# Second attention layer: the two parts of the output joined by VectorE out of PSUM

## The chip, the cores and the metric

The kernel runs on one core of one Trainium2 chip. The metric is the device time of one execution in microseconds. Three runs of the kernel before took 2756.7, 2753.62 and 2752.54 us; the median is 2753.62 us. One more execution was recorded by the hardware profiler: it took 2757.76 us, and the span from its first to its last instruction is 2756.0 us.

## The reference

All data are float32, the sequence has 1024 rows of 1024 channels. The reference computes a two-layer transformer block and then a state-space and convolution block. Each transformer layer is `x = x + g1 * attention(h)` and `x = x + g2 * swiglu(h)`, where `h` is an RMS norm of `x`, scaled and shifted by values that come from a conditioning vector.

The first layer has windowed attention (16 query heads, 4 key heads). The second, which the change touches, has dilated attention: three groups of 8 query heads and 2 key heads of 64 channels, with windows of 128, 512 and 2048 rows and dilations of 1, 4 and 16:

```python
for gi, (window, dil) in enumerate(B_GROUPS):
    half = window // (2 * dil)
    o, lse = banded_attention(to_strided(q[:, :, gi], dil), ...)
    outs.append(from_strided(o, b, dil)); lses.append(from_strided(lse, b, dil))
alpha = jax.nn.softmax(jnp.stack(lses), axis=0)
o = jnp.einsum('nbshg,nbshgd->bshgd', alpha, jnp.stack(outs))
```

Within a group each query attends to the keys at most `half` steps away in the strided sequence, with a bias that falls with the distance. The three groups' outputs are then weighed by the softmax of their log denominators, and a matrix multiplication follows.

## The kernel before

The program is one instruction stream per engine. The parts run one after the other: attention layer A, feed-forward 0, attention layer B (`layer_b`), feed-forward 1, the last block. Float32 products are made from operands split into a high part in the rounded format fp32r and the rest (`hi`, `lo`), so a projection is three matrix multiplications per tile (L590 to L592, into PSUM tiles `psg`), and a cast by ScalarE and a subtraction by VectorE make each split.

Layer B works through six units in the order of group 2, 1, 0 (dilations 16, 4, 1), two halves of the heads each. A unit has eight blocks of 128 queries for four heads, 48 blocks in all. A block goes through these steps (class `Block`, function `attend`):

- `score`: per head two matrix multiplications (L113, L114) into a PSUM bank of the two called `pssc`; VectorE adds the bias and takes the row maximum (L117), which frees the bank. After the fourth head VectorE scales the maxima (L122, 128x4).
- `soft`: ScalarE takes the exponential (L126) of each head, which needs L122.
- `turn`, one block later: TensorE transposes the four heads' weights P (L756) into a bank `pstp`; ScalarE casts the high part (L759), VectorE subtracts for the low part (L760).
- `apply`, also one block later (function `pv`): TensorE multiplies with the values (L770) into the only bank `pso`. The values stand there as high part and low part side by side, so the result has two parts: partitions 0 to 63 and 64 to 127 have to be added. ScalarE copies partitions 64 to 127 to an SBUF tile `ob` (L773) and partitions 0 to 63 to the output tile `o` (L779); GpSimd adds `ob` to `o` in place (L780).

The output tile holds a head's rows in their own order. In group 0 a block's 128 queries are 128 neighbours there. In group 1 they lie 4 elements apart and in group 2 16 apart, so the output of L779 is strided in the first four units and contiguous in the last two.

Between the steps `attend` calls `fill`, which issues pieces of the next unit's projections: the matrix multiplications, ScalarE's casts of the queries (L682), keys and values (L644 to L646, L659), VectorE's subtractions (L686, L648, L649, L660), and the next weights: a load on SyncE's queue (L544), a cast by ScalarE (L536), a subtraction by GpSimd (L537). The casts and subtractions of the queries and keys write strided in groups 2 and 1.

The outputs of groups 2 and 1 go to DRAM by SyncE when a unit is done (`spill`, L1125). Near the end of the layer the function `combine` (L1018 to L1060) reads them back and weighs the groups for one half of the rows, in small steps between the last blocks (L1031 and L1034 among them); the steps for the other half follow during the output projection.

The order on each engine's queue is not the written one. The program is traced, and the framework's scheduler sets the order of every queue at build time by what its own model of the run finds ready, what is written first being preferred; the run then keeps that order. Semaphores make an instruction wait, and what is behind it on its engine's queue waits with it. The function `pin` and the context `in_order` hold single places to the written order; layer B's blocks use neither.

The change touches the class `Net`'s start, the end of `pv`, and one line in `build`.

Of the kernel before, what the change touches and what calls it, by code (L numbers as in the profile page):

```python
# [32 lines left out]
class Steps:  # L33


    def __init__(self, gen):
        self.gen, self.value, self.live = gen, None, True
# [111 lines left out]
class Net:  # L149
    def __init__(self, tc, I, out, dbg=None):  # L150
        self.tc, self.nc, self.I, self.out = tc, tc.nc, I, out
        self.dbg = dbg or {}
        self.n = 0
        self.ready = {}
        self.spread_tag, self.sum_tag, self.ada_tag = "o", "r", "g"

    def nm(self, s):
# [476 lines left out]
    def kv_proj(self, W, h, perm, res):  # L634

        nc = self.nc
        K1, K2 = self.slab(dt=F32R, name="K1"), self.slab(dt=F32R, name="K2")
        vt = self.slab("tmp", name="vt")
        res.update(K1=K1, K2=K2, vt=vt)
        for hf in range(2):  # L640
            ps = self.bank("g")
            yield from self.col_gemm_steps(ps, W(), h, hf)
            pk, pv = perm(ps[0:64], None), perm(ps[64:128], None)
            nc.scalar.copy(perm(K1[0:64], hf), pk)  # L644
            nc.scalar.copy(perm(K1[64:128], hf), pk)
            nc.scalar.copy(perm(vt[64:128], hf), pv)  # L646
            yield
            nc.vector.tensor_sub(perm(K2[0:64], hf), pk, perm(fl(K1[0:64]), hf))  # L648
            nc.vector.tensor_sub(perm(K2[64:128], hf), pk, perm(fl(K1[0:64]), hf))  # L649
# [113 lines left out]
    def pv(self, pairs, oap, r0):  # L763

        nc = self.nc
        po = self.bank("o")
        n = len(pairs)
        for a, (v, pt) in enumerate(pairs):
            for part in range(2):
                nc.tensor.matmul(po, v, pt[:, part, :], start=(a == 0 and part == 0),  # L770
                                 stop=(a == n - 1 and part == 1))
        ob = self.small([P, H2], "ob", 2)[r0:r0 + 64]
        nc.scalar.copy(ob, po[64:128, :])  # L773
        a = po[0:64].rearrange("p (i q) -> p i q", i=4)
        b = ob.rearrange("p (i q) -> p i q", i=4)
        if len(oap.shape) == 4:
            r = oap.shape[2]
            a, b = [t.rearrange("p i (r q) -> p i r q", r=r) for t in (a, b)]
        nc.scalar.copy(oap, a)  # L779
        nc.gpsimd.tensor_add(oap, oap, b)  # L780

    def layer_a(self, h, late, then):
        nc, I = self.nc, self.I
# [1177 lines left out]
def build(tc, I, out, dbg=None, stop=None):  # L1961
    with ExitStack() as ctx:
        net, nc = Net(tc, I, out, dbg), tc.nc
        net.open(ctx)
        net.consts()
        net.load_vectors()
        xd, xd1 = net.spill_tile(), net.spill_tile()
        x0 = net.load_x(0)
        w1 = [net.ada_load(0, 1, k, "slab") for k in range(KT)]
        x1 = net.load_x(1)  # L1970
        w0 = [net.ada_load(0, 0, k, "slab") for k in range(KT)]
        net.x = Act(net, "x")
        with net.in_order():
            h, half = net.norm(net.x, lambda v: net.mod[0, 0] if v else s, rows=(x0, x1))
            first, second = Steps(half(0)), Steps(half(1))
            first.run(4)
            net.turn_x(0, x0)
            first.run(12)
            acc = net.ada_acc(w1)
            net.ada_fin(0, 1, acc)  # L1980
            s = net.ada_scale(0, 1, net.nmix[:, 0:8])
            first.run(1)
            second.run(4)
            net.turn_x(1, x1)
            acc = None
            for k in range(KT):
                acc = net.ada_acc(w0[:k + 1], acc, k)
                if k < 6:
                    second.run(2)
            for n, parts in enumerate(([(1024, 64), (1280, 64)], [(0, P)])):  # L1990
                net.ready[n] = net.load_cols(I["a_w_in"][0], parts, eng=nc.gpsimd)
            net.ada_fin(0, 0, acc)
            first.run()
            second.run()
        net.pending = second
        for hf in range(2):
            net.spill_x(xd, hf)
        net.half = {}

        def ffn_norm(i):  # L2000
            s2 = net.ada_scale(i, 4, net.nffn[:, 8 * i:8 * i + 8])
            net.H, half = net.block_norm(net.x, lambda v: net.mod[i, 3] if v else s2, lambda hf: net.spill_x(xd, hf))
            return half

        def b_norm():
            s = net.ada_scale(1, 1, net.nmix[:, 8:16])
            net.h, half = net.norm(net.x, lambda v: net.mod[1, 0] if v else s, ("s", "slab"))

            def both(hf, order=range(KT)):
                for n, _ in enumerate(half(hf, order)):  # L2010
                    if n == KT - 1:
                        net.spill_x(xd1, hf)
                    yield
            return both

        net.layer_a(h, lambda: net.reload_x(xd, True), lambda: ffn_norm(0))
        if stop == "A":
            return net.dump_x()
        early, late = net.ssm_params()
        net.ada_tag = "o"  # L2020
        d = net.ffn_wide(0, net.H, Steps(net.adas([(1, 1), (1, 0), (1, 2), (1, 4), (1, 3)], "wl")))
        net.ffn_narrow(0, d, xd, b_norm, early)
        if stop == "F0":
            return net.dump_x()
        net.layer_b(net.h, lambda: net.reload_x(xd1), lambda: ffn_norm(1))
        if stop == "B":
            return net.dump_x()
        d = net.ffn_wide(1, net.H, Steps(net.adas([(1, 5)], "wl")))
        net.ffn_narrow(1, d, xd, net.mix_norm, late)
        if stop == "F1":  # L2030
            return net.dump_x()
        net.mixer2()
# [41 lines left out]
```

## Time and profile before

| | before |
|---|---|
| median of three runs | 2753.62 us |
| the profiled execution's own time | 2757.76 us |
| its span | 2756.0 us |
| TensorE busy (matrix multiplications) | 2593.1 us, 94% |
| VectorE busy | 1899.1 us, 69% |
| ScalarE busy | 1286.1 us, 47% |
| GpSimd busy | 376.4 us, 14% |
| DMA, mean over the span | 122 GB/s |

Busy time is the time in which an engine works on an instruction; time in which it waits for a semaphore is idle. The shares are averages over stages of different kinds. In the rows further down, PE is TensorE's matrix multiplication and PEld its weight load, DVE is VectorE, ACT ScalarE, POOL GpSimd and SP SyncE. `out<-in` names the tiles that an instruction writes and reads, L779 is line 779 of the kernel, and a bracket such as `[1.08 <-PE pssc L114]` says how long the engine was idle before the instruction and which instruction ended that time. In a list of waits, the instruction on the left waited for the one on the right.

### The profile page before, as it was taken

The page shows a single profiled execution, that of the slowest core. Times are in us where ns is not written, and L with a number is a line of the kernel's source. Part 1 is how long each engine was busy: PE and PEld are TensorE (multiplying, and loading weights), DVE is VectorE, ACT ScalarE, POOL GpSimd, SP SyncE. Part 2 cuts the span into 40 slices and gives each one's busy share as a digit, 9 for nine tenths or more (in the row PEclk, how much of TensorE's full clock was granted, in tenths as well). Part 3 has the DMA queues.
Part 4 walks back from the last instruction along what each step waited for, and adds up shares of the span by engine and source line. Part 5 has one row for each costly group of instructions (what it writes and reads, how often), then busy time and mean ns, then how long its engine had stood idle before and what let it go on. Part 6 is the DMA issues. An engine that isn't in the chain of part 4 may idle for free. (4 is left out here: it accounts for less than half of the span.)

```text
span 2756.0 us, 33954 instructions
## 1 busy us (share of the span) xinstructions
PE 2593.1 (94%) x11966; PEld 2115.1 (77%) x11966; DVE 1899.1 (69%) x3559; ACT 1286.1 (47%) x2416; POOL 376.4 (14%) x506
## 2 busy tenths in 40 slices
PE   4999998999999999988899889999999899999998
PEld 4777676888888788776787668888887777988877
DVE  7788777977775976755667798666656978165355
ACT  4577743433333345568888443333333445123131
POOL 2255521000000000023343200000000102020000
PEclk8999999999999999999999999999999999999999
DMA  7333341544444666311122414222274565161141
GB/s 276 99 93 96 119 123 69 156 142 146 138 138 139 232 200 194 107 39 40 39 55 78 145 59 146 82 86 83 85 244 150 176 199 175 54 180 52 46 144 63
DMA packets 283403, 336.74 MB, mean 122 GB/s; under 512 B 59384, under 2 KB 212704, under 8 KB 282592
## 3 DMA queue, kind: packets, MB, share of 16 engines
q1 hardware_dynamic: 277520, 315.59, 36.4%
q0 software_dynamic: 5312, 18.88, 2.1%
q8 instruction: 94, 1.54, 0.2%
q14 instruction: 77, 0.63, 0.1%
q10 hardware_dynamic: 400, 0.09, 0.0%
HBM read 265.14 MB, written 67.27 MB: 121 GB/s over the span
## 5 line engine op out<-in xcount | busy, mean ns | idle before, releaser
L1188 PE MATMUL psg<-H,wpart 128*128 128x512 f32 x2112 | 504.6, 393 | 14.3 <-ACT H L432 10.0
L1188 PEld LDWEIGHTS psg<-H,wpart 128*128 128x128 f32 x2112 | 397.8, 189 | 103.6 <-ACT H L432 12.8
L1175 ACT CAST wpart<-wraw 128x512 fp32r<-128x512 f32 x264 | 163.3, 622 | 248.3 <-PE pstp L1188 76.4
L1188 PE MATMUL pssc<-H,wpart 128*128 128x512 f32 x1056 | 255.0, 390 | 0.5 <-DVE ev L1208 0.5
L1188 PEld LDWEIGHTS pssc<-H,wpart 128*128 128x128 f32 x1056 | 198.1, 188 | 42.1 <-DVE ev L1208 0.9
L1176 DVE TENSOR_TENSOR wpart<-wraw,wpart 128x512 fp32r<-128x512 f32 x264 | 180.9, 686 | 68.5 <-ACT wpart L1175 66.7
L1325 PE MATMUL psg<-part,wpart 128*128 128x512 f32 x792 | 206.8, 394 | 8.0 <-DVE wpart L1291 3.1
L1325 PE MATMUL pssc<-part,wpart 128*128 128x512 f32 x792 | 207.4, 394 | 5.2 <-DVE ev L1212 3.6
L590 PE MATMUL psg<-hh,wh 128*128 128x512 f32 x480 | 198.5, 414 | 2.2 <-ACT hh L527 1.7
L1290 ACT CAST wpart<-wraw 128x640 fp32r<-128x640 f32 (+1 forms) x132 | 101.0, 765 | 210.7 <-PE psg L1325 101.8
L591 PE MATMUL psg<-hl,wh 128*128 128x512 f32 x480 | 192.6, 401 | 2.0 <-DVE hl L530 1.9
L592 PE MATMUL psg<-hh,wl 128*128 128x512 f32 x480 | 191.8, 400 | 0.0
L1325 PEld LDWEIGHTS psg<-part,wpart 128*128 128x128 f32 x792 | 148.4, 189 | 42.7 <-DVE part L1297 5.5
L126 ACT ACTIVATE s<-s,nm 128x256 f32<-128x256 f32 (+4 forms) x320 | 162.4, 511 | 39.6 <-DVE nm L122 33.1
L1325 PEld LDWEIGHTS pssc<-part,wpart 128*128 128x128 f32 x792 | 148.3, 189 | 39.4 <-DVE ev L1212 4.3
L1291 DVE TENSOR_TENSOR wpart<-wraw,wpart 128x640 fp32r<-128x640 f32 (+1 forms) x132 | 117.7, 892 | 83.4 <-ACT wpart L1290 75.8
L1203 ACT COPY ev<-psg 128x512 f32<-128x512 f32 x132 | 77.4, 588 | 205.1 <-PE psg L1188 141.0
L780 POOL TENSOR_TENSOR o<-o,ob 64x512 f32<-64x512 f32 x80 | 117.3, 1467 | 231.8 <-ACT o L779 221.6
L403 POOL TENSOR_TENSOR nacc<-nacc,nsq 128x512 f32<-128x512 f32 x30 | 40.5, 1350 | 761.8 <-ACT nsq L401 761.5
L1325 PE MATMUL pstp<-part,wpart 128*128 128x512 f32 x528 | 137.9, 393 | 0.0
L1296 ACT CAST part<-a 128x512 fp32r<-128x512 f32 x176 | 108.5, 618 | 58.0 <-PE pssc L1325 17.7
L1297 DVE TENSOR_TENSOR part<-a,part 128x512 fp32r<-128x512 f32 x176 | 119.6, 691 | 19.0 <-ACT part L1296 17.8
(454 smaller groups left out, 5488.8 us busy)
## 6 DMA issues: line engine op xcount, KB each, us to landing
adaw<-in_ada_w_dram SPq DMA_DIRECT2D x96, 512.0 KB, 4.2
wraw<-in_ffn_w_in_dram SPq DMA_DIRECT2D x88, 512.0 KB, 3.9
a<-acts SPq DMA_DIRECT2D x132, 256.0 KB, 4.0
acts<-ev SPq DMA_DIRECT2D x44, 512.0 KB, 2.7
wraw<-in_ffn_w_out_dram SPq DMA_DIRECT2D x44, 384.0 KB, 3.5
xs<-x SPq DMA_DIRECT2D x32, 512.0 KB, 3.5
x<-xs SPq DMA_DIRECT2D x32, 512.0 KB, 5.1
wraw<-in_ffn_w_out_dram SPq DMA_DIRECT2D x44, 320.0 KB, 3.3
```

Source lines behind the costliest of these rows:

```text
L126: self.net.nc.scalar.activation(s[:, 0:w], s[:, 0:w], AF.Exp, bias=self.nm[:, i:i + 1], scale=0.125, accum_out=self.l[:, i:i + 1])
L590: nc.tensor.matmul(ps, hi[:, k, :], xhi, start=(k == 0), stop=False)
L591: nc.tensor.matmul(ps, hi[:, k, :], xlo, start=False, stop=False)
L592: nc.tensor.matmul(ps, lo[:, k, :], xhi, start=False, stop=(k == KT - 1))
L780: nc.gpsimd.tensor_add(oap, oap, b)
L1175: nc.scalar.copy(t[:, lo_half], src)
L1176: nc.vector.tensor_sub(t[:, hi_half], src, fl(t[:, lo_half]))
L1188: nc.tensor.matmul(bank[q, key], a[:, ks], b, start=first and k == m == 0, stop=k == 3 and m == 2, skip_group_check=not first)
L1291: nc.vector.tensor_sub(lo, t[:, 0:n], fl(hi))
L1296: nc.scalar.copy(o[:, lo_half], a)
L1297: nc.vector.tensor_sub(o[:, hi_half], a, fl(o[:, lo_half]))
L1325: nc.tensor.matmul(banks[m], a[:, ms], b, start=k == n == 0, stop=k == NK - 1 and n == 2)
```

## The change

A switch `sum_here` is added. `build` sets it before layer B, and from then on `pv` issues one VectorE addition of the two parts, the first read from PSUM and the second from `ob`, written to the output tile, in place of ScalarE's copy and GpSimd's addition. ScalarE's copy to `ob` stays. Layer A keeps the old form.

```diff
--- before.py
+++ after.py
@@ -152,6 +152,7 @@
         self.dbg = dbg or {}
         self.n = 0
         self.ready = {}
+        self.sum_here = False
         self.spread_tag, self.sum_tag, self.ada_tag = "o", "r", "g"
 
     def nm(self, s):
@@ -776,8 +777,11 @@
         if len(oap.shape) == 4:
             r = oap.shape[2]
             a, b = [t.rearrange("p i (r q) -> p i r q", r=r) for t in (a, b)]
-        nc.scalar.copy(oap, a)
-        nc.gpsimd.tensor_add(oap, oap, b)
+        if self.sum_here:
+            nc.vector.tensor_add(oap, a, b)
+        else:
+            nc.scalar.copy(oap, a)
+            nc.gpsimd.tensor_add(oap, oap, b)
 
     def layer_a(self, h, late, then):
         nc, I = self.nc, self.I
@@ -2022,6 +2026,7 @@
         net.ffn_narrow(0, d, xd, b_norm, early)
         if stop == "F0":
             return net.dump_x()
+        net.sum_here = True
         net.layer_b(net.h, lambda: net.reload_x(xd1), lambda: ffn_norm(1))
         if stop == "B":
             return net.dump_x()
```

## Rows read from the trace of the kernel before

**Rows 1.** Busy time of each engine in two stretches: the blocks of layer B, and the end of the layer. Columns: stretch, its length, busy us (and instructions) of PE, PEld, DVE, ACT and POOL, granted clock of TensorE, DMA share, GB/s.

```profile
1193.00:1545.00 352.00, 319.07 (x1649) 254.63 (x1648) 226.67 (x609) 284.19 (x661) 116.36 (x87) 0.98 0.22 54
...
1528.00:1545.00 17.00, 14.66 (x56) 8.72 (x56) 14.86 (x25) 9.08 (x22) 4.35 (x3) 1.00 0.50 169
```

**Rows 2.** The three longest waits of TensorE's matrix multiplications, 1193 to 1545 us. Columns: who waited for whom, us in total, times, longest us.

```profile
PE pso L770 <- DVE pt L760: 9.1, 12, 1.7
PE pssc L113 <- DVE st L117: 9.1, 10, 2.2
PE pso L770 <- ACT pt L759: 5.2, 9, 1.5
```

**Rows 3.** Instructions of one line: count, shortest, median and longest duration in ns, first and last start in us. L779 in groups 2 and 1 and then in group 0 (the first of its 17 is still of group 1), L686 in the first units and in the last, and L122 in layer B.

```profile
L779 ACT COPY o<-pso x31: 1012/1050/1092, 1204.8 to 1436.1; 64x512 f32<-64x512 f32 x31
...
L779 ACT COPY o<-pso x17: 577/581/1072, 1441.5 to 1539.7; 64x512 f32<-64x512 f32 x17
...
L686 DVE TENSOR_TENSOR Q<-psg,Q x16: 1007/1073/1106, 1169.1 to 1253.2; 64x512 fp32r<-64x512 f32 x16
...
L686 DVE TENSOR_TENSOR Q<-psg,Q x8: 683/689/694, 1472.0 to 1512.8; 64x512 fp32r<-64x512 f32 x8
...
L122 DVE TENSOR_SCALAR nm<-st x48: 150/484/3579, 1194.3 to 1527.1; 128x4 f32<-128x4 f32 x48
```

**Rows 4.** The group of GpSimd's additions, 1193 to 1545 us. Columns: count, busy us, mean ns of one, idle us before them and what ended it.

```profile
L780 POOL TENSOR_TENSOR o<-o,ob 64x512 f32<-64x512 f32 x48 | 71.1, 1481 | 209.0 <-ACT o L779 199.6 <-PE pstp L756 5.8 <-PE pssc L114 3.5
```

**Rows 5.** Timeline of VectorE, ScalarE and GpSimd in the block at 1390 us. Columns, here and below: start us, us, engine, line and operation, idle time before it.

```profile
1391.11 0.42 DVE L117 CUSTOM_DVE_ANT_0 s<-pssc,bias 128x256 f32<-128x256 f32 x1
...
1392.62 0.42 DVE L117 CUSTOM_DVE_ANT_0 s<-pssc,bias 128x256 f32<-128x256 f32 x1 [1.08 <-PE pssc L114]
...
1390.58 0.58 ACT L773 COPY ob<-pso 64x512 f32<-64x512 f32 x1 [0.21 <-PE pso L770]
...
1393.29 1.08 ACT L759 CAST pt<-pstp 128x512 fp32r<-128x512 f32 x2 [1.06 <-PE pstp L756]
...
1392.37 1.57 POOL L780 TENSOR_TENSOR o<-o,ob 64x512 f32<-64x512 f32 x1 [5.06 <-ACT o L779]
```

**Rows 6.** Timeline of the four engines in the block at 1226 us.

```profile
1228.71 3.58 DVE L122 TENSOR_SCALAR nm<-st 128x4 f32<-128x4 f32 x1
...
1233.36 0.69 DVE L760 TENSOR_TENSOR pt<-pstp,pt 128x512 fp32r<-128x512 f32 x1
...
1227.23 1.03 ACT L779 COPY o<-pso 64x512 f32<-64x512 f32 x1
1228.06 1.06 ACT L536 CAST wh<-wr 128x1024 fp32r<-128x1024 f32 x1
1229.03 2.21 ACT L682 CAST Q<-psg 64x512 fp32r<-64x512 f32 x2
1231.26 0.59 ACT L759 CAST pt<-pstp 128x512 fp32r<-128x512 f32 x1
...
1228.34 1.58 POOL L780 TENSOR_TENSOR o<-o,ob 64x512 f32<-64x512 f32 x1 [3.50 <-PE pssc L114]
1229.88 2.38 POOL L537 TENSOR_TENSOR wl<-wr,wh 128x1024 fp32r<-128x1024 f32 x1
...
1231.90 0.51 PE L770 MATMUL pso<-pt,V 128*128 128x512 f32 x1 [0.37 <-ACT pt L759]
...
1234.11 0.50 PE L770 MATMUL pso<-pt,V 128*128 128x512 f32 x1 [1.71 <-DVE pt L760]
```

**Rows 7.** Timeline of TensorE in five more blocks: matrix multiplications of L770 that waited for a half of the split.

```profile
1264.60 0.50 PE L770 MATMUL pso<-pt,V 128*128 128x512 f32 x1 [0.57 <-DVE pt L760]
...
1294.91 0.50 PE L770 MATMUL pso<-pt,V 128*128 128x512 f32 x1 [0.70 <-DVE pt L760]
...
1323.18 0.49 PE L770 MATMUL pso<-pt,V 128*128 128x512 f32 x1 [1.27 <-ACT pt L759]
1324.25 0.73 PE L770 MATMUL pso<-pt,V 128*128 128x512 f32 x2 [0.57 <-DVE pt L760]
...
1360.42 0.73 PE L770 MATMUL pso<-pt,V 128*128 128x512 f32 x2 [1.46 <-DVE pt L760]
...
1484.91 0.50 PE L770 MATMUL pso<-pt,V 128*128 128x512 f32 x1 [1.53 <-ACT pt L759]
```

**Rows 8.** Timeline of GpSimd, VectorE and TensorE at the first combine steps.

```profile
1519.02 1.30 POOL L780 TENSOR_TENSOR o<-o,ob 64x512 f32<-64x512 f32 x1 [4.43 <-ACT o L779]
...
1519.09 1.35 DVE L1031 TENSOR_TENSOR cE<-sn,cM 128x96 f32<-128x96 f32 x1
...
1522.99 0.25 DVE L1034 TENSOR_TENSOR cL<-cE,sn 128x96 f32<-128x96 f32 x1
...
1520.84 0.39 PE L113 MATMUL pssc<-K,Q 128*128 128x256 f32 x1 [1.18 <-DVE st L117]
```

**Rows 9.** Timeline of ScalarE, VectorE and TensorE in the block at 1242 us, and the last of the five places with the same wait.

```profile
1242.95 0.57 ACT L773 COPY ob<-pso 64x512 f32<-64x512 f32 x1
...
1242.81 2.11 DVE L686 TENSOR_TENSOR Q<-psg,Q 64x512 fp32r<-64x512 f32 x2 [2.53 <-ACT Q L682]
1244.95 0.29 DVE L117 CUSTOM_DVE_ANT_0 s<-pssc,bias 128x128 f32<-128x128 f32 x1
...
1245.30 0.39 PE L113 MATMUL pssc<-K,Q 128*128 128x256 f32 x1 [1.30 <-DVE st L117]
...
1408.51 0.39 PE L113 MATMUL pssc<-K,Q 128*128 128x256 f32 x1 [0.77 <-DVE st L117]
```

## Prediction, made before the change was run

> **What bounds the kernel now.** I read the page's share of each engine first: TensorE is busy for 94% of the span, VectorE for 69%, ScalarE for 47%, GpSimd for 14%. The edit acts only in the second attention layer, so I cut its stretch out by windows, 1193 to 1545 us. There TensorE is busy for 319.07 of 352.00 us, ScalarE for 284.19, VectorE for 226.67 and GpSimd for 116.36 [rows 1]. ScalarE, from which work is taken, is the second-fullest engine, and VectorE, which gets work, has some 125 us open. But the most that any edit of the other engines can bring is what TensorE stands idle: 32.9 us, or 1.2% of the run. So the question is what ends those 33 us.
>
> The list of waits says it. The output matmul (L770) waited 9.1 us in 12 places for VectorE's half of the split of P (L760) and 5.2 us in 9 for ScalarE's half (L759); the first score matmul (L113) waited 9.1 us in 10 places for VectorE's score add (L117) to free its PSUM bank [rows 2]. Twenty-two waits end on VectorE and nine on ScalarE. That is no plain gain: the change helps where ScalarE is late or where GpSimd holds VectorE up, and hurts where VectorE itself comes last.
>
> **What goes.** 48 ScalarE copies (L779), 31 of 1.05 us, whose output is strided (groups 2 and 1), and 17 of mostly 0.58 us [rows 3]: 31 x 1.05 + 17 x 0.58 = 42 us. And 48 GpSimd additions of 1.48 us mean, 71.1 us in all [rows 4].
>
> **What comes.** 48 VectorE additions of 64x512 with one operand in PSUM, one in SBUF. The nearest row is the query subtraction (L686), of the same shape and operands: 1.07 us with strided input and output, 0.69 us where both are contiguous [rows 3]. In the new addition only the output is strided, so 0.69 and 1.07 are its bounds in groups 2 and 1. I take 1.05, because a strided output alone already takes ScalarE's copy from 0.58 to 1.05. Sum: 31 x 1.05 + 17 x 0.69 = 44 us on VectorE. It costs as much as it replaces, on another engine; all hangs on where it falls.
>
> **The cover in a smooth block.** In the block at 1390 the copy to ob ends at 1391.16. VectorE is through with the first two score adds at 1391.53 and waits 1.08 us for the next scores [rows 5]. An addition of 1.05 us fits that gap. ScalarE, freed of its copy, only waits longer for the transposes, for which it already waits 1.06 us. So in smooth blocks the change is worth nothing, and costs nothing as long as the gap is there; without the gap each would cost 1.05 us.
>
> **Gains: heavy blocks.** In the block at 1226 ScalarE runs from ob without a pause through the o copy, a weight cast (L536) and two query casts before it comes to the split of P at 1231.26; TensorE waits 0.37 us for it. Meanwhile VectorE's small scaling of the row maxima (L122), 0.15 us at the least [rows 3], takes 3.58 us: from 1228.71 to 1232.29, across GpSimd's addition (1228.34 to 1229.92) and weight subtraction (L537, 1229.88 to 1232.26), ending with it. So the split's second half starts only at 1233.36, and TensorE waits 1.71 us [rows 6]. Without copy and addition ScalarE's half of the split comes 1.03 us sooner, and L536 ends near 1228.1, so that L537 holds L122 until about 1230.5, 1.8 us less. TensorE was ready at 1232.40 (1234.11 less its wait); L760 would be through before that. I count both waits as gone: 2.08 us. Five more places have this shape [rows 7]: 0.57 at 1264.60, 0.70 at 1294.91, 1.03 of the 1.84 at 1323.18 and 1324.25 (the copy's own length), 1.46 at 1360.42, and 1.4 of 1.53 at 1484.91. In the combine step a 128x96 subtraction (L1031) takes 1.35 us beside GpSimd's addition where a product of that shape (L1034) takes 0.25; TensorE's next wait is 1.18 us [rows 8], of which I count 1.1. Together 2.08 + 0.57 + 0.70 + 1.03 + 1.46 + 1.4 + 1.1 = 8.3 us.
>
> Can GpSimd hold the new addition too, as it holds L122? The score add at 1392.62, which also reads PSUM and SBUF, took its usual 0.42 us beside GpSimd's addition [rows 5], so I set that at nothing; held at the six meetings of L122 with L537 for up to 2.38 us [rows 6], it would be 14 us.
> The Trainium skill has the rule behind this ("SBUF — State Buffer", section "Who interferes with whom"): VectorE and GpSimd share a port pair, whoever takes it first keeps it for the whole instruction, and a VectorE instruction with one SBUF input, outside its two-port modes, does not contend. By that rule, too, the addition is never held, and L537 goes on holding L122; the trace agrees with both (0.42 us, and 3.58 us to the end of L537).
>
> **Losses: late blocks.** In the block at 1242 VectorE waits 2.53 us for ScalarE's query casts, does two subtractions in 2.11 us, and only then the score adds, at 1244.95; TensorE has waited 1.30 us for the bank. The copy to ob began at 1242.95 and took 0.57, so its data is there at 1243.52, before the subtractions end at 1244.92 [rows 9]. If the addition is queued at that place (it is written ahead of the next block's scores), all behind it on VectorE's queue, score adds, scaling, second half of the split, comes 1.05 us later, and TensorE with it. Behind the scores it costs nothing. There are five places of this kind, the waits at 1245.30 and 1408.51 the first and last [rows 9]: between 0 and 5 x 1.07 = 5.4 us. Nothing in the trace of before tells the place, so I take half, 2.7 us.
>
> At the end of the layer (1528 to 1545) VectorE is busy for 14.86 of 17 us [rows 1], and three additions of 0.69 us, 2.1 us, meet 2.1 us of room that is not all in the right place: half of it, 1.0 us, to the cost.
>
> **Transfers and banks.** The spills of groups 2 and 1 now wait for VectorE in place of GpSimd; what they write is read back only at the end of the layer. SyncE's queue holds weight loads behind GpSimd's L537, which comes sooner or at the same time. L770's PSUM bank (one buffer) was free at the end of the o copy and is now free at the end of the addition; the next L770 comes only after the next block's scores, transposes and projections. I set these at nothing; the last costs if an addition is queued that late.
>
> **Sum.** -8.3 + 2.7 + 1.0 = -4.6 us. The profiled execution took 2757.76 us around its span of 2756.0, so it would become 2753.2; it lies 4.1 us over the median of the runs, 2753.62, which becomes 2749.0.
>
> **Rivals.**
> - *The additions hold nothing up.* All fall into gaps as at 1390: -8.3 + 1.0 = -7.3 us, 2746.3. For it: VectorE has the room. Against it: the block at 1242.
> - *No difference.* All five late blocks pay, 5.4 us, and some 1.5 us of the gains go where the wait that ends bares the next one: -8.3 + 5.4 + 1.0 + 1.5 = -0.4, 2753.2. For it: the two kinds of block stand side by side, so what one gains the next can lose. Against it: in the heavy blocks two engines come sooner at once.
> - *VectorE becomes the last at every place.* One mechanism: the addition waits at the head of VectorE's queue for the ob copy, which ScalarE makes late, and the scores wait behind it. It decides from the point where an addition stands in front of work that TensorE already waits for; that work exists in 22 places [rows 2], six of which go with the gains. 16 x 1.07 - 8.3 + 1.0 = +9.8 us, 2763.4. For it: VectorE waits 2.53 us behind ScalarE in just this way at 1242.81. Against it: the addition would have to stand in front each time, while in smooth blocks it has its gap.
>
> **How the numbers follow.** 0.38 for the forecast (2744 to 2753), 0.24 for the first rival, 0.18 for no difference, 0.20 for the slower one. A measurement of this kernel tells about 0.2%, 5.5 us, from no change: faster is under 2748.1, slower over 2759.1. Of the forecast's 0.38 some 0.17 lie under 2748.1 and 0.21 in between; the first rival gives 0.20 and 0.04; no difference 0.01 under, 0.15 within and 0.02 over; the slower rival 0.02 within and 0.18 over. Faster 0.38, same 0.42, slower 0.20. The range runs from 2741 (the first rival and 5 us of the waits left uncounted) to 2762, almost the slower rival.
>
> **What would show it.** In the changed profile L122's median falls from 0.48 us [rows 3] towards 0.17, with long ones only beside L537; the new addition reads 1.0 to 1.1 us in groups 2 and 1 and 0.69 in group 0; ScalarE's busy time in the layer falls by 42 us. L770's waits shrink by some 7 us, L113's waits for L117 grow by up to 5. I am wrong if the addition reads far from 1.05, if L113's wait grows past what L770 gains, or if the scheduler orders the layer anew, so that blocks no longer match one for one.

## The result and the profile after

The changed kernel takes 2768.93 us (median of 11 runs) against 2753.67 for the kernel before, a ratio of 1.0052 (95%: 1.0039 to 1.0066). In a second set of runs it was 1.0034 (1.0022 to 1.0046). It is slower, by 9 to 15 us, where 4.6 us less were forecast; the time lies above the range. The profiled execution took 2767.7 us around a span of 2766.0.

Blocks are counted below from 0 to 47 in the order of the layer: 0 to 15 group 2, 16 to 31 group 1, 32 to 47 group 0. "The layer" is the stretch from the end of block 0's last L770 (L771 after the change) to that of block 47, and a block's own stretch, for which its idle time is given, runs from the end of its last L770 to that of the next block: there its addition stands. Two rows of the windows view, columns as in [rows 1]; before:

```profile
1204.12:1539.01 334.89, 303.58 (x1589) 243.34 (x1588) 217.57 (x585) 275.42 (x638) 115.09 (x86) 0.98 0.21 48
```

and after:

```profile
1205.47:1547.89 342.42, 305.44 (x1591) 244.71 (x1590) 240.24 (x632) 235.40 (x591) 45.40 (x39) 0.99 0.21 48
```

ScalarE gives up 40 us, GpSimd 70, VectorE takes only 23 more (the additions are 44.5, and its small operations are held less: L122 alone takes 16.4 us in place of 33.9). TensorE's idle time, length less busy time, grows from 334.89 - 303.58 = 31.31 us to 342.42 - 305.44 = 36.98. This difference is the measure used below, for a reason told in the last section. Where the idle time went is in the list of waits, which answers to [rows 2]; after, 1194 to 1557 us:

```profile
PE pssc L113 <- DVE st L117: 15.7, 21, 2.1
PE pso L771 <- DVE pt L761: 8.0, 12, 1.5
PE pssc L113 <- DVE Q L687: 3.0, 4, 1.4
...
PE pso L771 <- ACT pt L760: 2.6, 5, 1.3
PE pso L771 <- DVE o L781: 1.7, 4, 0.6
```

The waits for ScalarE's half of the split fell from 5.2 to 2.6 us and those for VectorE's half from 9.1 to 8.0. The waits for the score add rose from 9.1 us in 10 places to 15.7 in 21, and the output matmul has a new wait of 1.7 us for the addition to free its bank. The two groups of instructions that the prediction named (count, shortest, median and longest ns):

```profile
L781 DVE TENSOR_TENSOR o<-pso,ob x48: 672/1036/1084, 1206.5 to 1550.6; 64x512 f32<-64x512 f32 x48
...
L122 DVE TENSOR_SCALAR nm<-st x48: 150/170/2370, 1195.6 to 1539.4; 128x4 f32<-128x4 f32 x48
```

The addition is as long as forecast, and L122 is freed as forecast (0.17 us in place of 0.48 [rows 3]). So the price did not fail, and L122 got its relief; how little of that reached TensorE comes below. Three timelines of after show what failed. A smooth block, the one that answers to [rows 5]:

```profile
1395.79 0.58 ACT L774 COPY ob<-pso 64x512 f32<-64x512 f32 x1 [1.09 <-PE pso L771]
...
1395.97 0.42 DVE L117 CUSTOM_DVE_ANT_0 s<-pssc,bias 128x256 f32<-128x256 f32 x1 [1.63 <-PE pssc L114]
...
1396.43 1.07 DVE L781 TENSOR_TENSOR o<-pso,ob 64x512 f32<-64x512 f32 x1
...
1397.54 0.42 DVE L117 CUSTOM_DVE_ANT_0 s<-pssc,bias 128x256 f32<-128x256 f32 x1
...
1398.03 0.39 PE L113 MATMUL pssc<-K,Q 128*128 128x256 f32 x1 [0.23 <-DVE st L117]
```

VectorE does not run the two score adds and then the addition in its 1.08 us of room. The addition stands between the first and the second score add, the second comes some 1.1 us later, and with it the PSUM bank for TensorE's next scores: 0.23 us of idle time where there was none. A late block, which answers to [rows 9]:

```profile
1241.72 2.12 DVE L687 TENSOR_TENSOR Q<-psg,Q 64x512 fp32r<-64x512 f32 x2 [2.53 <-ACT Q L683]
...
1241.86 0.57 ACT L774 COPY ob<-pso 64x512 f32<-64x512 f32 x1
...
1243.87 1.01 DVE L781 TENSOR_TENSOR o<-pso,ob 64x512 f32<-64x512 f32 x1
1244.73 0.26 DVE L117 CUSTOM_DVE_ANT_0 s<-pssc,bias 128x128 f32<-128x128 f32 x1
...
1245.06 0.39 PE L113 MATMUL pssc<-K,Q 128*128 128x256 f32 x1 [1.92 <-DVE st L117]
```

The addition is ahead of both score adds; TensorE waits 1.92 us in place of 1.30. And the heavy block of [rows 6]:

```profile
1228.98 1.06 DVE L781 TENSOR_TENSOR o<-pso,ob 64x512 f32<-64x512 f32 x1 [0.42 <-ACT ob L774]
...
1230.44 0.17 DVE L122 TENSOR_SCALAR nm<-st 128x4 f32<-128x4 f32 x1
...
1230.53 2.20 ACT L683 CAST Q<-psg 64x512 fp32r<-64x512 f32 x2
1232.75 0.59 ACT L760 CAST pt<-pstp 128x512 fp32r<-128x512 f32 x1
...
1230.58 2.40 POOL L538 TENSOR_TENSOR wl<-wr,wh 128x1024 fp32r<-128x1024 f32 x1 [13.12 <-PE pstp L757]
```

Here L122 takes 0.17 us where it took 3.58, and is over before the weight subtraction begins. Block 3's idle time falls from 2.07 us to 0.84.

Over the first 32 blocks the addition stands ahead of both score adds in six (1, 5, 9, 13, 18, 26), between the two in thirteen (16 to 31 without 18, 22 and 26), and behind the second in the other thirteen. The scheduler also set TensorE's own queue in another order, one of the signs of being wrong that the prediction names: in the six blocks some of the transposes now come ahead of scores, in 6 and 25 a score or a product has moved, and from block 32 on the order differs throughout. Those last blocks stood idle for 8.36 us before and 8.90 after, so nearly all of the loss lies in the first 32.

So there were gains, and there were losses; the experiments are there to tell which is whose.

### The profile page after: what moved, and what is told of

It is laid out like the page before. It is cut to its first block, busy times and chain, and to the rows that moved or that the text cites. A ratio compares the mean times of both kernels' runs of the same rounds, so it can differ in the third digit from the quotient of the medians.

```text
span 2766.0 us, 33917 instructions
## 1 busy us (share of the span) xinstructions
PE 2597.3 (94%) x11966; PEld 2116.4 (77%) x11966; DVE 1922.1 (69%) x3607; ACT 1244.9 (45%) x2368; POOL 304.8 (11%) x458
## 5 line engine op out<-in xcount | busy, mean ns | idle before, releaser
L760 ACT CAST pt<-pstp 128x512 fp32r<-128x512 f32 x168 | 93.1, 586 | 106.7 <-PE pstp L757 105.3
L1300 ACT CAST part<-a 128x512 fp32r<-128x512 f32 x176 | 108.5, 618 | 58.1 <-PE pssc L1329 16.4
L1192 PE MATMUL pstp<-H,wpart 128*128 128x512 f32 x528 | 130.5, 394 | 1.3 <-ACT H L428 0.7
```

The costliest lines, as they stand in the source:

```text
L1192: nc.tensor.matmul(bank[q, key], a[:, ks], b, start=first and k == m == 0, stop=k == 3 and m == 2, skip_group_check=not first)
L1300: nc.scalar.copy(o[:, lo_half], a)
```

## The experiments

Ratios are against the kernel before, timed in the same set of runs. The theories of the first four: P, the addition's place in VectorE's queue makes the loss; L, VectorE's added load makes it, wherever it stands; N, the relief is never worth anything.

**Behind the second score add.** The addition is written behind the next block's first two scores, and ordered behind them without a semaphore.

```
-            nc.vector.tensor_add(oap, a, b)
+            return lambda: nc.vector.tensor_add(oap, a, b)
...
                 b.score(0)
                 b.score(1)
+                self.marked()
+            self.finish(bool(b))
```

> Each addition is queued on VectorE behind the second score add of the next block, never between the two or ahead of them. Theory P (the place in VectorE's queue is what costs): L113's waits for L117, 14.4 us in the changed kernel, fall to the 9 us of the kernel before or under; the late blocks still scale their maxima later, so about half of the loss against the kernel before goes and the gains of the heavy blocks stay: 2750 to 2757 us. Theory L (VectorE's load of 44 us is what costs, wherever it stands): 2764 to 2770, as the changed kernel. Theory N (there never was a gain from the ScalarE copies and GpSimd additions that went): not under 2754 anywhere.

Measured 2756.66 us, ratio 1.0005 (0.9995 to 1.0014): the loss is gone. In the trace VectorE's order in a smooth block is now the one that the prediction took for granted, and TensorE does not wait:

```profile
1382.22 0.42 DVE L117 CUSTOM_DVE_ANT_0 s<-pssc,bias 128x256 f32<-128x256 f32 x1 [0.82 <-PE pssc L114]
...
1382.57 0.42 DVE L117 CUSTOM_DVE_ANT_0 s<-pssc,bias 128x256 f32<-128x256 f32 x1
...
1383.03 1.08 DVE L799 TENSOR_TENSOR o<-pso,ob 64x512 f32<-64x512 f32 x1
1384.14 0.43 DVE L117 CUSTOM_DVE_ANT_0 s<-pssc,bias 128x256 f32<-128x256 f32 x1
```

The waits for the score add are down to 5.9 us; the layer's idle time is 29.72 us, 1.6 under the kernel before:

```profile
1201.18:1531.84 330.66, 300.94 (x1591) 242.63 (x1590) 240.10 (x632) 235.38 (x591) 45.46 (x39) 0.99 0.21 50
...
PE pso L789 <- DVE pt L779: 9.8, 13, 1.7
PE pssc L113 <- DVE st L117: 5.9, 9, 1.3
```

VectorE does the same work as in the changed kernel (240.10 us in 632 instructions in the layer, there 240.24 in 632), ScalarE too. In their queues only the addition's place differs, so P holds, and L falls as the cause of the whole loss. Two things limit that. In the six blocks where the addition had stood ahead of the scores TensorE's order changed with it, back to scores first; of the 7.3 us of idle time that the run takes away 4.1 lie there, and the two are not told apart, while the other 3.1 lie in blocks where TensorE's order is the same. And blocks 14, 17, 22, 27, 30 and 34 still stand 0.6 to 1.2 us above the kernel before, 4.5 us together, so the added work costs something in this place too. That it is no faster than before leaves N open.

**Later still, behind the second half of the split.** The same, with the mark set behind L760's subtraction in place of the second score.

```
         nc.vector.tensor_sub(pt[0:n, 1, :], tpf[0:n], fl(pt[0:n, 0, :]))
+        self.marked()
```

> Each addition is queued on VectorE behind the subtraction of the split of P in the next block, where VectorE's next work waits for the next output matmul. P: nothing that TensorE waits for stands behind it, so only the gains are left: 2744 to 2750. L: 2764 to 2770. N: 2753 to 2756. If the one PSUM bank of the output matmul comes free too late there, L770 waits for the addition, up to 1 us in 48 places.

Ratio 1.0039 (1.0027 to 1.0052), idle time 39.13 us. The waits for the score add are as in the run before, but the one PSUM bank of the output matmul now comes free too late:

```profile
1204.07:1551.26 347.19, 308.06 (x1606) 248.29 (x1605) 242.72 (x637) 236.26 (x592) 45.47 (x39) 0.98 0.22 53
...
PE pso L789 <- DVE o L799: 13.7, 9, 2.8
PE pssc L113 <- DVE st L117: 5.7, 8, 1.3
PE pso L789 <- DVE st L117: 4.9, 2, 2.6
```

The time, 2767.43 us, is the one expected under L, and P's 2744 to 2750 did not come; but L gives no reason for the new wait, and P had named it as the exception. So the place has an end on both sides: behind the second score add, before the split.

**Only in the blocks 3 and 7 of the first four units.**

```
+            here = g > 0 and qb in (3, 7)
...
+        self.net.sum_here = self.here
```

> VectorE adds only in the blocks 3 and 7 of each of the first four units (8 of 48); elsewhere ScalarE copies and GpSimd adds as before. P: the gains of the heavy blocks (about 6 us of the 8.3 counted) without the losses: 2747 to 2750. L: 8 of 48 of the loss, 2756. N: 2754 to 2756.

Ratio 0.9992 (0.9982 to 1.0003), not clear of noise, and idle time 29.19 us. Blocks 3, 15 and 19 give 1.29, 1.00 and 0.81 us of idle time back; blocks 23, 27 and 31, smooth ones of group 1, take 0.34, 0.31 and 0.33. The relief is real where there was a stall, and the misplaced addition costs in these three smooth blocks.

**A shorter addition.** The changed kernel with the permutation of the output left out, so that the addition is 0.69 us everywhere.

```
-                oap = og.rearrange("p i (a r) -> p i a r", r=4)[:, :, a0:a0 + P, r]
+                oap = og[:, :, qb * P:(qb + 1) * P]
```

> The changed kernel with the output of groups 2 and 1 written in the order of the queries: it leaves the permutation out. The queue's order is that of the changed kernel, the addition takes 0.69 in place of 1.04 us. P: in the smooth blocks of group 1 the second score add then comes in time (0.23 us of wait and some 0.25 us of delay behind it go, in about 9 blocks), the late ones gain 0.35 each: 2760 to 2763. L: the time goes with the load, 31 x 0.35 = 11 us: 2757 to 2759. N: no statement.

Ratio 1.0012 (1.0003 to 1.0021), idle time 30.48 us:

```profile
1208.15:1541.24 333.09, 302.61 (x1592) 243.34 (x1590) 228.56 (x632) 235.56 (x591) 45.38 (x39) 0.99 0.21 50
```

TensorE's order is that of the changed kernel in every block. In the same place, an addition 0.36 us shorter in groups 2 and 1 takes 6.5 us of idle time away, and the 0.23 us of the smooth blocks 16, 20, 24 and 28 are gone. The time, 2758.29 us, is in L's range and under P's; the 6.5 us of idle time are nearer to P's 6 to 9 than to L's 11, so the run does not decide between the two. Place and length act together: in those four blocks the shorter addition fits the room at its place.

**The changed kernel again, without an edit.**

> The changed kernel once more, on the chip of the following ones. Its profile shows +7.5 us in the second attention layer, its runs a median +15.3 us. If the layer is all of the loss, the ratio is 1.0027 (+7.5 of 2755) and the loss of the first comparison was partly the chip's own spread; if something beyond the layer is slower too, it stays at 1.0045 to 1.006, and a second trace shows in which stage. Inside the layer both expect the same table: blocks 5 and 13 +2.2 us each (two of it clock or the copy's order), 16, 20, 24, 28 +0.5 each, 3 and 15 -1.0 to -1.25.

Ratio 1.0034, idle time 37.22 us (36.98 in the first trace), the same block by block to 0.2 us. The layer's length, though, is +4.4 us here and +7.5 there. The difference is TensorE's clock: of the stretches granted 0.50 (1.2 GHz), one falls into the layer here, three there and in the kernel before.

**Nine blocks, behind the second score add.** The order of the first experiment, only in blocks that had gained by it.

```
+HERE = {1, 3, 9, 13, 15, 18, 19, 25, 26}
...
+        self.net.g, self.net.sum_here = self.g, self.k in HERE
```

> The addition by VectorE, queued behind the second score add, only in the nine blocks of 48 that gained in e1_behind_scores (1, 3, 9, 13, 15, 18, 19, 25, 26); the other 39 keep copy and GpSimd addition. If the gains are each block's own: 0.36 + 1.25 + 0.80 + 0.25 + 1.01 + 1.1 + 0.50 + 0.28 + 1.08 = -6.6 us against the kernel before, 2748.5, ratio 0.9976. If a block's gain hangs on the blocks beside it (GpSimd's weight subtraction moved by their additions), some of it is lost: -2 to -4 us, 2751 to 2753. If nothing is ever gained: 2755, ratio 1.000.

Measured 2751.41 us against 2758.03, ratio 0.9975 (0.9964 to 0.9986): faster than both kernels. The layer's idle time is 25.03 us, 6.3 less than before:

```profile
1208.52:1535.18 326.66, 301.63 (x1590) 242.39 (x1588) 216.15 (x594) 267.48 (x629) 101.23 (x77) 0.99 0.21 50
```

The sum came out as expected, 6.3 us for 6.6, but in part by luck. The nine blocks gained 4.2 us: 1, 13 and 18 nothing, 9 only 0.29. The rest came in blocks that keep the old form: 2 and 10, the ones behind 1 and 9, gained 0.70 and 0.55 us, 38 gained 0.59, and 43 gained 1.26: there the combine step's subtraction (L1031 in the kernel before, 1.35 us) now ran 0.25 us and was over before GpSimd's addition began.

```profile
1515.66 0.25 DVE L1057 TENSOR_TENSOR cE<-sn,cM 128x96 f32<-128x96 f32 x1
...
1516.62 1.29 POOL L806 TENSOR_TENSOR o<-o,ob 64x512 f32<-64x512 f32 x1 [4.43 <-ACT o L805]
```

The six blocks that stood above the kernel before in the first experiment are back at it.

**The same nine, left where the scheduler puts them.**

```
+                self.finish(False)
                 b.score(0)
                 b.score(1)
-                self.marked()
-            self.finish(bool(b))
```

> The nine blocks of f4_nine_blocks, but the addition left where the scheduler puts it, as in the changed kernel. If the place decides also where ScalarE's relief gains, each block does as in the trace of the changed kernel: 1 +0.39, 3 -1.23, 9 +0.16, 13 +0.6, 15 -1.03, 18 -0.65, 19 -0.49, 25 -0.28, 26 -0.40, sum -2.9 us, about 3.5 us more than f4: ratio 0.9989. If the place costs only in the other 39 blocks: as f4, ratio 0.9975.

Ratio 0.9989 (0.9979 to 0.9998), idle time 27.84 us. Blocks 1, 9, 13, 18 and 26, where the addition stands ahead of the scores, lose 3.6 us against the run before, of which the other blocks give 0.8 back. So the place decides in these blocks as well, together with TensorE's order, which differs from the run before in these five blocks alone. From the changed kernel's 36.98 us the choice of blocks alone takes 9.1, the order alone 7.3 (first experiment), and both together 12.0.

**Whose is the relief?** Seven kernels add to the first experiment what one engine had given up: a copy of the old shape and output stride by ScalarE, or an addition by GpSimd, with a result that is used nowhere (so). In all of them VectorE's addition is behind the second score add. In the first pair so is the free half of the ob tile:

```
+            so = obt[64 - r0:128 - r0].rearrange("p (x r) -> p r x", r=r)
+            nc.scalar.copy(so, po[0:64].rearrange("p (r x) -> p r x", r=r))
             return lambda: nc.vector.tensor_add(oap, a, b)
```

or, in place of the copy,

```
+            y = ob.rearrange("p (r x) -> p r x", r=r)
+            nc.gpsimd.tensor_add(so, y, y)
```

This pair put the extra work into the first attention layer too, and VectorE's addition with it, so that only the second layer can be read from them (ratios 1.0027 and 1.0041). Theory S has the gain come from ScalarE's time, theory G from GpSimd's, which ends the hold on L122.

> The addition queued behind the second score add (as in e1_behind_scores), but ScalarE does a copy of the old length (64x512 out of PSUM, same output stride, into a spare half tile) behind the ob copy, as in the kernel before. GpSimd stays freed. Theory S (the gain is ScalarE's time): the blocks that gained in e1 (3: -1.25, 9: -0.80, 15: -1.01, 18: -1.1, 26: -1.08) return to the kernel before, so the layer is some 5 us longer than e1's, 2760. Theory G (the gain is GpSimd's, which ends the hold on VectorE's scaling): these gains stay and the layer is within 1 us of e1's, 2756 to 2757.

> As e1_behind_scores, but GpSimd does an addition of the old shape (64x512, strided output, result left unused) when ob is there. ScalarE stays freed. Theory G: VectorE's scaling L122 is held again (median 0.4 to 0.5 us in place of 0.17, long ones of 2 to 3.5 us), block 3 loses 1.2 us of its gain and the layer 3 to 5 us; near 2760. Theory S: L122 is held again, but the blocks 9, 15, 18, 26 keep their gains, so the layer is within 1.5 us of e1's; 2756 to 2758.

Idle time in the layer 35.75 us with the copy kept and 30.02 with GpSimd's addition kept. The second told nothing of a hold: GpSimd had its operand a copy's length sooner than in the kernel before, and L122 kept its 0.17 us. The next pair is confined to the layer, and GpSimd's line stands twice.

> f2_scalar_kept with the extra copy in the second attention layer alone (there it ran in the first layer too, so that only its second layer could be compared: +6.7 us against the kernel before, e1 -4.2). Theory S: the layer again some 10 us longer than e1's, and now the whole time too: 2763 to 2767, ratio 1.003 to 1.0045. If the layer's 10 us do not come back in the whole time (a later stage hides them): 2756 to 2758.

> e1_behind_scores with two additions of the old shape by GpSimd, one behind the other, when ob is there, in the second attention layer alone: GpSimd is taken until some 3 us after the ob copy, where in the kernel before it was until some 2.5 us (one addition in f3_gpsimd_kept came 1.05 us sooner than before and held nothing). Theory G: L122 is held again (median 0.4 to 0.5 us) and the weight subtraction comes late as before; the layer is 4 to 6 us longer than e1's, block 3 keeps at most 0.4 of its 1.25 us; ratio 1.002. Theory S: L122 is held, but blocks 9, 15, 18, 26 keep their gains and block 3 at least 0.8; the layer is at most 2 us longer than e1's; ratio 1.000 to 1.001.

Ratio 1.0032 (1.0020 to 1.0045), idle time 34.97 us with the copy; 1.0023 (1.0013 to 1.0032) and 31.85 us with the two additions. Both have a flaw. The two additions were 1.07 us each, 2.15 together, less than the 2.5 that was meant. And VectorE's addition waited for the extra copy as well: idle 21.1 us before 27 of 48. A third pair gives so a tile of its own and makes GpSimd's second addition one of the old form.

```
-            so = obt[64 - r0:128 - r0].rearrange("p (x r) -> p r x", r=r)
+            so = self.small([P, H2], "scr", 1)[r0:r0 + 64].rearrange("p (x r) -> p r x", r=r)
...
-            nc.gpsimd.tensor_add(so, y, y)
+            nc.gpsimd.tensor_add(so, so, y)
```

> g1_scalar_kept_2, but ScalarE's extra copy goes to a tile of its own (the ob tile then has one buffer in place of two): in g1 it went to the free half of the ob tile, and the addition waited for it too (21.1 us before 27 of 48, in e1 some 6 before 11). So g1's 10 us more of layer than e1 are ScalarE's time and the addition's delay together. Theory S: the delay is not what counts; TensorE's idle time in the layer stays near g1's 35.0 us (e1 29.7), block 15 keeps none of its gain, blocks 25, 27, 30 lose 1.0 to 1.4 us; ratio 1.0025 to 1.004. The delay counts: idle time 30 to 32 us, ratio 1.0005 to 1.0015.

> g2_gpsimd_twice with GpSimd's two additions longer (1.07 and some 1.5 us, the second of the old form, in a tile of its own), so that it is taken until 2.5 us after the ob copy, as in the kernel before; in g2 it was 2.15 us, and L122 was held to a median of 0.26 us against 0.48 before. Theory S: L122 is held more than in g2, yet blocks 3, 9, 15 and 18 keep 0.8 us or more each, TensorE's idle time in the layer is under 33.5 us (g2 31.9, e1 29.7, before 31.3); ratio 1.001 to 1.0025. Theory G: blocks 3 and 9 fall back to the kernel before, idle time 34 us or more, ratio over 1.0025.

A tile of its own did not end the wait (21.1 us before 25), so the copy's destination is not the cause: ratio 1.0018, idle time 34.75 us, and nothing new. The GpSimd run is clear: ratio 1.0056 (1.0039 to 1.0072), idle time 37.98 us. L122 is back at 0.45 us, and in block 3 at 3.64, across GpSimd's second addition and the weight subtraction (L544 here) behind it:

```profile
1197.65:1543.28 345.63, 307.65 (x1591) 245.86 (x1590) 260.24 (x632) 235.91 (x591) 166.50 (x133) 0.98 0.20 48
...
1223.00 1.58 POOL L807 TENSOR_TENSOR scr<-scr,ob 64x512 f32<-64x512 f32 x1
...
1223.30 3.64 DVE L122 TENSOR_SCALAR nm<-st 128x4 f32<-128x4 f32 x1
...
1224.54 2.37 POOL L544 TENSOR_TENSOR wl<-wr,wh 128x1024 fp32r<-128x1024 f32 x1
```

Blocks 3 and 19 lose all their gain (2.14 and 2.15 us idle, before 2.07 and 1.46), as theory G has it; block 15 keeps its own (0.81), as S has it.

The last of the seven lets the copy read ob:

```
-            nc.scalar.copy(so, po[0:64].rearrange("p (r x) -> p r x", r=r))
+            nc.scalar.copy(so, ob.rearrange("p (r x) -> p r x", r=r))
```

> h1_scalar_kept_3, but ScalarE's extra copy reads ob in place of the PSUM bank (in h1 the addition still waited for it, 21.1 us before 25 of 48, although it had a tile of its own). Now the addition should wait for the ob copy alone, as in e1 (some 6 us before 11), and only ScalarE's 42 us are added. Theory S (ScalarE's time is part of the gain): block 15 keeps none of its 1.0 us and block 26 half; idle time of TensorE in the layer 32 to 34.5 us (e1 29.7). If the delay alone made the loss of g1 and h1: blocks 15 and 26 keep their gains, idle time 29.5 to 31 us, ratio 1.0005.

The addition now waits for the ob copy alone (7.4 us before 15), and ScalarE's time is the only thing added. The copies, the layer, and the wait that comes back:

```profile
L805 ACT COPY scr<-ob x48: 606/1092/1153, 1205.8 to 1541.8; 64x512 f32<-64x512 f32 x48
...
1205.14:1541.10 335.96, 303.18 (x1593) 242.29 (x1591) 235.95 (x633) 280.83 (x639) 45.59 (x39) 0.99 0.22 53
...
PE pso L793 <- ACT pt L782: 6.1, 10, 1.3
```

Ratio 1.0016 (1.0006 to 1.0027), idle time 32.78 us. The waits for ScalarE's half of the split are back at 6.1 us, where the first experiment had 2.7. Block 15 is back at 1.85 us, 19 at 1.22, block 3 keeps most (1.19), and block 26 keeps all of its gain, where theory S had it lose half. So the relief has two parts. ScalarE's is 32.78 - 29.72 = 3.1 us of idle time at most: 1.4 us of it lie in the first 32 blocks, and the other 1.7 in the last ones, where TensorE's order differs between the two kernels in half of the blocks. GpSimd's is at most 37.98 - 29.72 = 8.3, at most because GpSimd's two additions last 2.65 us where the one before lasted 1.48.

TensorE's idle time per block, us, where the kernels differ most:

| block | before | after | e1 behind scores | f4 nine blocks | h3 ScalarE's time kept | h2 GpSimd's time kept |
|---|---|---|---|---|---|---|
| 3 | 2.07 | 0.84 | 0.81 | 0.78 | 1.19 | 2.14 |
| 15 | 1.84 | 0.82 | 0.84 | 0.83 | 1.85 | 0.81 |
| 19 | 1.46 | 0.69 | 0.94 | 0.91 | 1.22 | 2.15 |
| 5 | 1.30 | 1.92 | 1.30 | 1.52 | 1.31 | 1.29 |
| 13 | 1.56 | 2.15 | 1.31 | 1.55 | 1.44 | 1.65 |
| 14 | 0.49 | 1.55 | 1.72 | 0.50 | 1.68 | 1.73 |
| 22 | 0.00 | 0.71 | 0.69 | 0.00 | 0.74 | 0.91 |
| 24 | 0.00 | 0.23 | 0.00 | 0.00 | 0.00 | 0.00 |
| 30 | 0.18 | 1.31 | 0.86 | 0.18 | 0.93 | 0.97 |
| layer | 31.31 | 36.98 | 29.72 | 25.03 | 32.78 | 37.98 |

## Why the prediction was wrong

In the layer's idle time the forecast's -4.6 us became +5.7: the gains came to 3.7 for 8.3, the smooth blocks cost 2.0 for nothing, and all other blocks together 7.4 for 3.7. Its own sign of being wrong came: the first score matmul's wait for the score add grew by 6.6 us, while the output matmul's waits shrank by 2.0, from 14.3 to 12.3 with the new one.

*What comes* was right: 1.05 us in groups 2 and 1 and 0.68 in group 0, 44.5 us in all where 44 were worked out. The addition was never held by GpSimd: its longest is 1.084 us, and 1.121 in the run that kept GpSimd busiest. The rule cited from the Trainium skill ("SBUF — State Buffer", section "Who interferes with whom") says the same, and the 3.64 us of L122 agree with its other half, though there the hold goes through two GpSimd instructions in a row. *What goes* was right (ScalarE 40 us less).

*The cover in a smooth block* failed. The gap of 1.08 us was there, but the step never asked whether the addition would stand at it. It did not: in blocks 16, 20, 24, 27, 28, 29 and 31 the addition came before the second score add, for 0.22 to 0.49 us each, 2.0 us together, where nothing was counted. The text priced the missing gap (1.05 us a block) but not the wrong order. The clue was in [rows 5]: the ob copy ends at 1391.16, just as the second score add begins, so the addition's data can be there before that score's turn.

*Losses: late blocks* failed in the count. Half of five places was taken, 2.7 us. The waits for the score add rose by 6.6 us, from 10 places to 21. Of the five, blocks 5, 13 and 21 lost 0.6 to 0.7 us each, while 18 and 26 gained; but 14, 17, 22, 23, 30 and 34 lost 0.7 to 1.1 each, four of which had waited 0.2 us or less. In 14, 22 and 34 the new wait is not for the score add: the addition stands behind it, and TensorE waits for VectorE's half of the split, which comes later. At the end of the layer, where 1.0 us was counted, blocks 44 to 46 lost 0.1 together. A list of present waits shows the places without slack, not those with less slack than the addition's 1.05 us.

*Gains: heavy blocks* had the right mechanism and a sum too large. Of the 8.3 us, in the order of the prediction: block 3 gave 1.24 for 2.08, block 7 0.07 for 0.57, block 11 0.13 for 0.70, block 15 1.02 for 1.03, block 19 0.77 for 1.46, block 37 lost 0.22 for a gain of 1.4, and the combine step in block 43 gave 0.71 for 1.1: 3.7 us. Block 15, the copy's own length, came to 0.01 us. The places where two engines had to come sooner at once gave half or nothing. In the heavy block above the weight cast did not come 1.03 us sooner, as the step has it, but stood still for 0.51 us; it began 0.08 us after TensorE's last product with the weights that the cast's tile had held before (`psg<-hl,wh`):

```profile
1228.98 0.39 PE L592 MATMUL psg<-hl,wh 128*128 128x512 f32 x1
...
1229.45 1.05 ACT L537 CAST wh<-wr 128x1024 fp32r<-128x1024 f32 x1 [0.51 <-issue]
```

In the kernel before the same product ended at 1227.64, so there the cast, at 1228.06, could have begun at most 0.42 us sooner:

```profile
1227.25 0.39 PE L591 MATMUL psg<-hl,wh 128*128 128x512 f32 x1
```

ScalarE's half of the split then began 4.39 us after the start of the ob copy, before 4.62: 0.23 us sooner in place of 1.03, and TensorE waits 0.70 us for VectorE's half behind it. The profile names no releaser for the 0.51 us; the product is inferred from the two times. And the weight subtraction, where it comes sooner, can meet L122 in another place: L122 took 2.37 us in block 11 (before 1.22) and 1.92 in block 27 (0.51).

*Transfers and banks* was set at nothing "if" the addition is not queued late. As changed it costs 1.7 us in four places at the end of the layer; queued behind the split, 13.7.

Of the rivals, *VectorE becomes the last at every place* named the mechanism, with 2763.4 us. Its condition, an addition in front of work that TensorE waits for, holds in the late blocks and half holds in the smooth ones; most single places cost less than the 1.07 us counted, and there were more of them. The predicted sign hung on the order in a queue, which the trace of the kernel before does not hold. The forecast treated the order as half a loss in five places; it should have been carried through all 48. But the order alone does not make the forecast right: with every addition of the first four units behind the second score add the layer gained 1.6 us, not the 7.3 of the rival *The additions hold nothing up*.

The layer's idle time explains 5.7 us of the 9 to 15. In the two traces the span is 10.0 and 10.2 us longer than before: 5.7 and 5.9 are idle time in the layer, 4.2 and 2.0 are TensorE's busy time over the whole span, with the same matrix multiplications, and 0.1 and 2.2 are idle time outside the layer, in stages whose code is the same. In the first trace 116.6 us of the span are granted 0.50, before 108.2; half of these 8.4 us is an estimate of what a busy TensorE loses by it, and it is the 4.2. Whether the edit has a part in that, or single executions differ so, stays open. The layer begins 1.35 us (2.1 in the second trace) late, and the kernels of the experiments begin it between 6.5 us early and 4.4 late, the two that change the first layer aside.

## What to carry to other kernels

Moving work to an engine with room was decided here more by where it was queued than by the room: find for each block the instruction that it will stand in front of, who waits for that, and whether the slack there is longer than the added work, the places that wait for nothing today included. Then make the order explicit, here behind the second score add, and use the edit only in the blocks whose stall it ends; the same edit went from 0.5% slower to 0.25% faster. Relief of a busy engine is real, but what stands next in the chain can take it back: of 8.3 us counted 3.7 came, and in full only where the wait was one operation long. So look, for each freed instruction, at what else it waits for.

## What was not expected

A place too late cost more than one too early: idle time 39.13 us behind the split, 36.98 where the scheduler put it (in 19 of the first 32 blocks ahead of the scores or among them), 29.72 behind the second score add.

An addition waited for a copy that it shares nothing with but the PSUM bank that both read: 21.1 us before 25 of 48 additions, gone (7.4) when the copy read from SBUF. Whether that is a wait that the framework adds or one of the bank itself was not tried.

TensorE's clock moves the length of a stretch without any change in its work, in lumps. After the change one of the layer's stretches at half clock is (columns as in [rows 1])

```profile
1246.60:1249.80 3.20, 3.20 (x9) 2.52 (x8) 0.69 (x1) 1.58 (x9) 0.00 (x0) 0.50 0.24 10
```

and before it was at 1234.9 us, in another block. TensorE is busy in it without a pause, so blocks 5 and 13 seem to lose 2.2 us each in one trace of the changed kernel and 0.6 in the other, with the same idle time (1.92 and 1.93, 2.15 and 2.16). That is why idle time, not length, is compared here.
